# A two-layer decoder step in fp32: how the convolution's taps are spread over the stages, which units stand beside a layer's first blocks, and narrower attention operands

## The chip, the core and the metric

The kernel runs on one core of one Trainium2 chip. The metric is the device time of one execution in microseconds (us), as the median of several runs. The engines are named as in the profile: PE (TensorE matmul) and PEld (its weight loads), DVE (VectorE), ACT (ScalarE), POOL (GpSimd) and SP (SyncE, which issues DMAs).

## What is computed

One inference step of a decoder with two layers, for a prompt of 1024 tokens and 8 sampled sequences of 4 tokens: 1056 token columns in all, model width 1024, everything in float32. Cut to what matters here:

```
h = rms(x)*(1+scale) + shift                       # scale, shift from an adaLN product
u_a, bch, glu, q, k, v, mgate, mrg = split(h @ w_in)
y_a = pooled means over windows 2/4/8/16, minus self, times w_pool          # A
y_b = B * dwconv3(C * h_b)                                                   # B
y_c = silu(layernorm(dwconv31(val*sigmoid(gl)) + b))                         # C
w   = softmax(q1 k1) - lam * softmax(q2 k2);  y_d = rms(w @ v)               # D, causal, 4 heads
merged = sum_n sigmoid(mrg_n) * ((y_n * silu(mgate_n)) @ w_branch_n)
x = x + gate * rms(merged @ w_o)
```

`lam` is exp(lq0.lq1) - exp(lq2.lq3) + a constant, from a small input. The samples attend to 1024 cached tokens each, and the convolutions and the pooling take their past rows from small state inputs.

## The kernel before

**Products.** Channels lie on the 128 partitions and tokens along the free axis, in three blocks of 352 columns (the last holds 320 prompt columns and the 32 sample columns). Each fp32 operand is split into a high part (copied to the fp32r format, L208 for weights on ACT) and a remainder (L209 on DVE); a product is three matmul series, high*high, high*low and low*high (`three`), so an item of eight 128-row slices is 24 matmuls of 352 columns (`gemm`, L236). A *unit* is one 128-channel slice of the input projection for all three blocks, so three items. `Ring` loads a unit's weights two ahead and splits them into three pairs of buffers (whi, wlo); `rmain.dest` can name other tiles for a unit.

**Order.** `drive` runs a list of units: for each item the matmuls, then the evaluation of its PSUM block, one `step_side` (two more inside the item) and `fills[n % len(fills)]` calls of `step_fill`. `side` holds generators whose work is laid between the items: one attention head (`attn`), the decoding of two heads (`decode`), `pool`, `layernorm`. `fill` holds the taps of branch C. Each engine runs its instructions in one fixed order, so an instruction that waits holds up all behind it.

**A layer.** `layer` first runs the first head's K, V and Q units for blocks 0 and 1, then starts `attn(0)`, runs block 2 of the three units, and goes on with the gate of branch D (`mgd(0)`) and branch B. The previous layer's output projection makes the third block's input last: its sum of squares (`sumsq`, L366 to L373: ACT squares, DVE `tensor_reduce`), the reciprocal root (`rstd_of`, whose matmul is L354), and `norm_apply` (L388 DVE, L389 ACT, L390 DVE). In layer 0 `rstd_x` does the sum of squares by eight fp32 matmuls with ones (L1260). `setup_lambda` loads the input of `lam` into the tile `od` (L417), and its exponential is L420 on ACT. The heads 1 to 3 follow in turn with the rest of branch B beside them; the last is attention 3.

**Attention.** For a query block of 128 rows `a_part` makes scores S for two maps (q, k: matmul, mask matmul, remainder matmul with `kl`), the row maximum (L582), the exponential (L585) and the difference of the two maps. The columns of a chunk are at least 256 (`chunks`). `t_part` transposes the weights, and `pv` (L614) multiplies pairs of query blocks by V; where the first block of a pair can see nothing of a key block, a memset puts zeros there. At the end L351 to L362 normalise the head.

**Branches A and C.** `ev_val` makes the convolution's input, and `conv` appends 32 entries per channel slice c to `fill`: `samples`, then 31 taps, each one DVE instruction over 128x1024 (L947). The units gl(0) to gl(2) come first, then four pairs `ua(c)`, `mga(c)` (the pooling units, each with `pool(c)`: window sums on POOL L1006, DVE L1013, ACT L1014, DVE L1015, three small products, L1023 to L1025), then gl(3). `FR = (2,)`: two fills per item in all of them and in the merges. After gl(3) the loop runs fills until no `samples` stands in front and not all 32 entries of slice 3 are left. The four merges follow in the order A, B, D, C; what is left in `fill` runs in the first one and at its end (`drain_fill`). The layer norm of branch C (L1081, L1084, L1088) runs beside the third merge.

```
            if sides:
                step_side()
            step_fill(fills[n % len(fills)])
...
        drive(first, order=[(u, b) for b in range(2) for u in range(3)], begun=begun)
        side.append(attn(0))
        drive(first, order=[(u, 2) for u in range(3)])
        drive([mgd(0), uc_(0), uh(0), ub(0)])
```

## Time and profile before

| | |
|---|---|
| median of 3 runs | 2972.73 us (2972.08 to 2975.25) |
| the profiled execution | 2971.34 us, span of its work 2969.6 us |
| PE busy | 2882.3 us, 97% |
| DVE, ACT, POOL busy | 1618.5, 1060.0, 483.1 us (55%, 36%, 16%) |
| mean granted TensorE clock | 0.989 of full speed |

An engine's busy time is the time in which one of its instructions ran. Times in rows count from the start of the span. A matmul's own duration in a row holds a latency that overlaps with its neighbours; what it takes of PE is the distance from its start to the next start. The granted clock of a stretch is the mean over it, 1.00 being the upper of the two levels and 0.5 the lower.

### The profile page before, as it was taken

The page shows a single profiled execution, that of the slowest core. Times are in us where ns is not written, and L with a number is a line of the kernel's source. Part 1 is how long each engine was busy: PE and PEld are TensorE (multiplying, and loading weights), DVE is VectorE, ACT ScalarE, POOL GpSimd, SP SyncE. Part 2 cuts the span into 40 slices and gives each one's busy share as a digit, 9 for nine tenths or more (in the row PEclk, how much of TensorE's full clock was granted, in tenths as well). Part 3 has the DMA queues.
Part 4 walks back from the last instruction along what each step waited for, and adds up shares of the span by engine and source line. Part 5 has one row for each costly group of instructions (what it writes and reads, how often), then busy time and mean ns, then how long its engine had stood idle before and what let it go on. Part 6 is the DMA issues. An engine that isn't in the chain of part 4 may idle for free.

```text
span 2969.6 us, 45889 instructions
## 1 busy us (share of the span) xinstructions
PE 2882.3 (97%) x18198; PEld 2774.0 (93%) x18198; DVE 1618.5 (55%) x2488; ACT 1060.0 (36%) x2086; POOL 483.1 (16%) x632
## 2 busy tenths in 40 slices
PE   7999999999999999999979999999999999999997
PEld 5999898999899999999979988988999999999997
DVE  5766366489952145323487653675799422543233
ACT  5565256322112133213455652653221121322132
POOL 1121010113100111011230110201140001220123
PEclk9999999999999999999999999999999999999999
DMA  6114621551232233222321245116411221221122
GB/s 237 51 58 134 186 64 39 177 158 45 81 110 101 72 104 102 79 72 72 111 97 48 73 148 174 57 36 198 141 41 60 81 72 50 77 87 58 50 70 98
DMA packets 135960, 280.06 MB, mean 94 GB/s; under 512 B 18338, under 2 KB 88994, under 8 KB 134210
## 3 DMA queue, kind: packets, MB, share of 16 engines
q10 hardware_dynamic: 45072, 145.74, 15.7%
q1 hardware_dynamic: 79778, 90.73, 9.6%
q0 software_dynamic: 10896, 40.67, 3.7%
q8 instruction: 143, 2.34, 0.3%
q14 instruction: 71, 0.58, 0.1%
HBM read 240.73 MB, written 36.34 MB: 93 GB/s over the span
## 4 chain that ended last, share of the span: by engine, by line
PE 80%; DVE 7%; ACT 5%; DMA 3%; SPq 3%; issue 2%; POOL 0%; ACTq 0%; DVEq 0%; POOLq 0%
PE mm_t L236 42%; PE m_t L236 28%; PE s_t L236 3%; DVE acc_t L947 2%; SPq L664 2%; PE ms_t L236 2%; PE ms_t L603 1%; DMA e_t<-in_kc_dram 1%; ACT rop_t L489 1%; SPq L401 1%; DVE wlo_t L209 1%; PE s_t L769 1%; PE s_t L695 1%; PE ada_t L298 1%; PE ms_t L1260 1%
## 5 line engine op out<-in xcount | busy, mean ns | idle before, releaser
L236 PE MATMUL mm_t<-hh_t,whi_t 128*128 128x352 f32 x2792 | 528.9, 327 | 10.8 <-ACT hh_t L383 4.8
L236 PE MATMUL mm_t<-hh_t,wlo_t 128*128 128x352 f32 x2792 | 528.6, 326 | 0.0
L209 DVE TENSOR_TENSOR wlo_t<-wst_t,whi_t 128x1024 fp32r<-128x1024 f32 x203 | 269.2, 1330 | 475.9 <-ACT whi_t L208 475.3
L236 PE MATMUL mm_t<-hl_t,whi_t 128*128 128x352 f32 x2792 | 525.3, 325 | 0.0
L236 PEld LDWEIGHTS mm_t<-hh_t,whi_t 128*128 128x128 f32 x2792 | 460.2, 190 | 22.9 <-issue 7.5
L236 PEld LDWEIGHTS mm_t<-hl_t,whi_t 128*128 128x128 f32 x2792 | 462.0, 189 | 11.2 <-issue 10.0
L236 PEld LDWEIGHTS mm_t<-hh_t,wlo_t 128*128 128x128 f32 x2792 | 463.0, 190 | 4.1 <-issue 3.3
L947 DVE SCALAR_TENSOR_TENSOR acc_t<-uc_t,vec_t,acc_t 128x1024 f32<-128x1024 f32 x240 | 319.2, 1346 | 2.0
L208 ACT ACTIVATE whi_t<-wst_t 128x1024 fp32r<-128x1024 f32 x203 | 213.4, 1056 | 275.6 <-PE mm_t L236 194.1
L1158 POOL TENSOR_TENSOR mg_t<-mg_t,th_t 128x352 f32<-128x352 f32 x144 | 145.3, 1011 | 932.9 <-DVE th_t L1157 932.7
L236 PE MATMUL m_t<-hh_t,wlo_t 128*128 128x352 f32 x1352 | 248.5, 325 | 0.0
L236 PE MATMUL m_t<-hl_t,whi_t 128*128 128x352 f32 x1352 | 248.2, 325 | 0.0
L236 PE MATMUL m_t<-hh_t,whi_t 128*128 128x352 f32 x1352 | 246.1, 324 | 0.7 <-DVE ga_t L979 0.7
L236 PEld LDWEIGHTS m_t<-hh_t,wlo_t 128*128 128x128 f32 x1352 | 224.3, 190 | 0.6
L236 PEld LDWEIGHTS m_t<-hl_t,whi_t 128*128 128x128 f32 x1352 | 224.2, 190 | 0.2
L236 PEld LDWEIGHTS m_t<-hh_t,whi_t 128*128 128x128 f32 x1352 | 222.9, 189 | 1.0 <-DVE ga_t L979 1.0
L1065 ACT ACTIVATE th_t<-m_t 128x352 f32<-128x352 f32 x114 | 52.7, 463 | 376.3 <-PE m_t L236 372.4
L1065 ACT ACTIVATE th_t<-mm_t 128x352 f32<-128x352 f32 x78 | 36.0, 463 | 262.3 <-PE mm_t L236 254.4
L585 ACT ACTIVATE e_t<-s_t,sml_t 128x256 f32<-128x256 f32 (+7 forms) x128 | 94.2, 739 | 51.7 <-DVE sml_t L583 50.7
L582 DVE TENSOR_REDUCE sml_t<-s_t 128x1 f32<-128x256 f32 (+7 forms) x128 | 94.0, 751 | 12.4 <-PE s_t L236 11.6
L236 PE MATMUL m_t<-yh_t,whi_t 128*128 128x352 f32 x460 | 94.6, 326 | 0.0
L236 PE MATMUL m_t<-yl_t,whi_t 128*128 128x352 f32 x460 | 93.2, 324 | 0.0
(361 smaller groups left out, 3928.0 us busy)
## 6 DMA issues: line engine op xcount, KB each, us to landing
wst_t<-in_wst_dram ACTq DMA_DIRECT2D x209, 512.0 KB, 3.7
e_t<-in_kc_dram SPq DMA_DIRECT2D x224, 128.0 KB, 2.9
e_t<-in_vc_dram SPq DMA_DIRECT2D x216, 128.0 KB, 2.8
rld_t<-ysp_t ACTq DMA_DIRECT2D x16, 528.0 KB, 4.1
wa_t<-in_wada_dram SPq DMA_DIRECT2D x16, 512.0 KB, 9.2
wlo_t<-in_wada_dram ACTq DMA_DIRECT2D x16, 512.0 KB, 3.7
whi_t<-in_wada_dram ACTq DMA_DIRECT2D x16, 512.0 KB, 4.3
x_t<-in_xT_dram SPq DMA_DIRECT2D x3, 1408.0 KB, 12.9
```

The source lines that it names most:

```text
L208: sc.activation(out=R(hi), in_=st, func=AF.Copy)
L209: (eng or ve).tensor_tensor(out=R(lo), in0=st, in1=hi, op=ALU.subtract)
L236: last_mm[0] = m = te.matmul(out=out, lhsT=R(lh), rhs=R(rh), start=first and i == 0, stop=last and i == n - 1)
L298: te.matmul(out=acc[c:c + 32], lhsT=scs[:, k], rhs=w, start=k < 4, stop=k >= 4)
L401: r = sp.value_load(pt[0:1, i:i + 1], min_val=0, max_val=NPOOL - 1)
L489: sc.activation(out=sw[32 * (g ^ 1):32 * (g ^ 1) + 32], in_=pb[32 * g:32 * g + 32], func=AF.Copy)
L582: ve.tensor_reduce(out=s[:, j:j + 1], in_=S[j][:, :n], axis=AX.X, op=ALU.max)
L585: sc.activation(out=E[qb % 2][j][:, :n], in_=S[j][:, :n], func=AF.Exp, bias=s[:, 2 + j:3 + j], scale=0.125, accum_out=s[:, 4 + j:5 + j])
L664: sp.dma_start(out=buf[:, j * 256:(j + 1) * 256], in_=cache[l][bass.ds(r, 1), p].rearrange("a p n -> p (a n)"))
L947: pace(ve.scalar_tensor_tensor(out=a, in0=v, scalar=w(k), in1=a, op0=ALU.mult, op1=ALU.add))
L1065: sc.activation(out=th[:, b * TB:(b + 1) * TB], in_=pb, func=AF.Tanh, scale=0.5)
L1158: gp.tensor_tensor(out=mg[:, d, cl], in0=mg[:, d, cl], in1=th, op=ALU.add)
```

## The change

Seven edits, in one diff:

- `fold` replaces every `tensor_reduce` over the middle axis by two `tensor_tensor` additions (704 and 352 columns), in `sumsq` and twice in `layernorm`; `rstd_x` does blocks 1 and 2 so, with one fp32 matmul in place of eight.
- `mgd(0)` becomes the fourth unit of the first group: after blocks 0 and 1 of K, V and Q come the three items of `mgd(0)`, then block 2 of K, V and Q. The weights of `mgd(0)` go to the tiles `od` and `e7`. While it runs, `attn(0)` stops before its third query block.
- A chunk of S takes only the columns it has; `pv` multiplies only the 128 live columns for the last key block of a pair, and its memsets go.
- `od` and `ms` change places in `decode`, and `od` is allocated in `pv(0)`, the tiles e4 to e7 in the first `t_part`.
- Sample columns of branch C have their own tile and DMA.
- Two fills per item stay in the gl units; one in the pooling units; 3, 2, 3 for the items of a unit in the merges.
- The loop after gl(3) runs only while a `samples` entry stands in front, which `appendleft` now puts there as soon as it exists.

```diff
@@ -362,13 +362,17 @@
-    def sumsq(x, t, acc):
+    def fold(t, out, first=None):
+        h = t[:, 0:2] if first is None else first
+        ve.tensor_tensor(out=h, in0=t[:, 0:2], in1=t[:, 2:4], op=ALU.add)
+        ve.tensor_tensor(out=out, in0=h[:, 0], in1=h[:, 1], op=ALU.add)
+    def sumsq(x, ts, acc):
...
-            k = slice(4 * i, 4 * i + 4)
-            o = t[:, k] if t.shape[1] == KC else t
-            sc.activation(out=o, in_=x[:, k], func=AF.Square)
-            ve.tensor_reduce(out=acc[:, i], in_=o.rearrange("p k n -> p n k"), axis=AX.X, op=ALU.add)
+            sc.activation(out=ts[i], in_=x[:, 4 * i:4 * i + 4], func=AF.Square)
+            fold(ts[i], acc[:, i])
@@ -551,10 +555,9 @@
-            wt = [ep(f"e{4 + i}", 4, 256) for i in range(4)]
-            od = ep("od", 1056)
-            qz = ep("ms", 1024)[:, 0:512].rearrange("p (i j q) -> p i j q", i=2, j=2)
+            wt, od = [], []
+            qz = ep("ms", 1056)[:, 0:512].rearrange("p (i j q) -> p i j q", i=2, j=2)
@@ -566,7 +569,7 @@
-                chunks = [slice(c0, c0 + min(512, max(n - c0, 256))) for c0 in range(0, n, 512)]
+                chunks = [slice(c0, min(c0 + 512, n)) for c0 in range(0, n, 512)]
@@ -591,10 +594,9 @@
             def t_part(qb):
+                if qb == 0:
+                    wt.extend(ep(f"e{4 + i}", 4, 256) for i in range(4))
...
-                if qb % 2 == 0:
-                    for lo in range(2):
-                        gp.memset(wtp(lo, qb + 1)[:, 0:P], 0.0)
@@ -607,17 +609,23 @@
-                pr = []
-                for k in range(2 * s + 2):
-                    pr += [(vh[:, k], wtp(0, k)), (vh[:, k], wtp(1, k)), (vl[:, k], wtp(0, k))]
-                gemm(pb, pr)
-                sc.activation(out=od[:, s * 256:s * 256 + 256], in_=pb, func=AF.Copy)
+                pr = [(v, lo, k) for k in range(2 * s + 2) for v, lo in ((vh, 0), (vh, 1), (vl, 0))]
+                pr = pr[:-4] + pr[-3:] + pr[-4:-3]
+                for i, (v, lo, k) in enumerate(pr):
+                    c = slice(P if k == 2 * s + 1 else 0, 256)
+                    gemm(pb[:, c], [(v[:, k], wtp(lo, k)[:, c])], first=i == 0, last=i == len(pr) - 1)
+                if s == 0:
+                    od.append(ep("od", 1056)[:, :SEQ])
+                sc.activation(out=od[0][:, s * 256:s * 256 + 256], in_=pb, func=AF.Copy)
...
                 while qb >= 5 and kqdone[h] < 2 or qb >= 7 and not vdone[h]:
+                    yield
+                while qb == 2 and held:
                     yield
@@ -856,18 +864,23 @@
-        first = kvq(0)
+        gq = Pool(f"gq{l}", LEFT, reuse_waits="tile")
+        first = kvq(0) + [mgd(0)]
+        rmain.dest[pos[first[3][0]]] = [ep(t, n)[:, 0:1024] for t, n in (("od", 1056), ("e7", 1024))]
+        held.append(True)
...
+        drive(first, order=[(3, 0), (3, 1), (3, 2)])
+        held.clear()
...
-        gq = Pool(f"gq{l}", LEFT, reuse_waits="tile")
-        drive([mgd(0), uc_(0), uh(0), ub(0)])
+        drive([uc_(0), uh(0), ub(0)])
@@ -928,34 +941,38 @@
             def samples():
-                a = st["a"] = cpool("acc", T)
+                a = cpool("smp", NS)
...
-                    ve.tensor_reduce(out=a[:, SEQ + i:SEQ + i + 16], in_=prd, axis=AX.X, op=ALU.add)
-                ve.tensor_scalar(out=a[:, SEQ:], in0=a[:, SEQ:], scalar1=cv("b_cconv", l, c), scalar2=None, op0=ALU.add)
+                    ve.tensor_reduce(out=a[:, i:i + 16], in_=prd, axis=AX.X, op=ALU.add)
+                ve.tensor_scalar(out=a, in0=a, scalar1=cv("b_cconv", l, c), scalar2=None, op0=ALU.add)
+                gp.dma_start(out=csp[l, c, :, SEQ:], in_=a)
...
                 def f():
-                    a, v = st["a"][:, 0:SEQ], u[:, k:k + SEQ]
+                    if k == 0:
+                        st["a"] = cpool("acc", SEQ)
+                    a, v = st["a"], u[:, k:k + SEQ]
...
-                        gp.dma_start(out=csp[l, c], in_=st["a"])
+                        gp.dma_start(out=csp[l, c, :, 0:SEQ], in_=a)
...
-            fill.append((c, samples))
+            fill.appendleft((c, samples))
...
-        FR = (2,)
+        FC, FA, FM = (2,), (1,), (3, 2)
...
-        drive(gl(0) + gl(1) + gl(2), 1, FR)
+        drive(gl(0) + gl(1) + gl(2), 1, FC)
@@ -1028,16 +1045,16 @@
-        drive([ua(0), mga(0)], 1, FR)
+        drive([ua(0), mga(0)], 1, FA)
...
-            drive([ua(c), mga(c)], 1, FR)
-        drive(gl(3)[:1], 1, FR)
+            drive([ua(c), mga(c)], 1, FA)
+        drive(gl(3)[:1], 1, FC)
...
-        drive(gl(3)[1:], 1, FR)
+        drive(gl(3)[1:], 1, FC)
...
-        while fill and fill[0][1].__name__ == "samples" or sum(t == 3 for t, _ in fill) == 32:
+        while fill and fill[0][1].__name__ == "samples":
@@ -1078,14 +1095,14 @@
-                ve.tensor_reduce(out=s1, in_=x.rearrange("p k n -> p n k"), axis=AX.X, op=ALU.add)
+                fold(x, s1, t[:, 0:2])
...
-                ve.tensor_reduce(out=s2, in_=t.rearrange("p k n -> p n k"), axis=AX.X, op=ALU.add)
+                fold(t, s2)
@@ -1137,7 +1154,7 @@
-                    drive([win(O_MRG + n * D, 2 * dp + x, ev_mrg(ths[x]))], 1, FR)
+                    drive([win(O_MRG + n * D, 2 * dp + x, ev_mrg(ths[x]))], 1, FM)
@@ -1253,15 +1270,20 @@
-            for i in range(2):
-                tx = su("tx", 4, TB, bufs=2)
-                sc.activation(out=tx, in_=xb0[b][:, 4 * i:4 * i + 4], func=AF.Square)
-                for k in range(4):
-                    te.matmul(out=pb, lhsT=ones, rhs=tx[:, k], start=i + k == 0, stop=i + k == 4)
+            ts = [su("tx", 4, TB, bufs=2) for _ in range(2)]
+            if b == 0:
+                for i in range(2):
+                    sc.activation(out=ts[i], in_=xb0[b][:, 4 * i:4 * i + 4], func=AF.Square)
+                    for k in range(4):
+                        te.matmul(out=pb, lhsT=ones, rhs=ts[i][:, k], start=i + k == 0, stop=i + k == 4)
+            else:
+                te.matmul(out=pb, lhsT=ones, rhs=sumsq(xb0[b], ts, accs[b]), start=True, stop=True)
...
-            ve.scalar_tensor_tensor(out=t, in0=pb, scalar=-3.0, in1=y, op0=ALU.add, op1=ALU.mult)
+            rs = t if b < 2 else pb
+            ve.scalar_tensor_tensor(out=rs, in0=pb, scalar=-3.0, in1=y, op0=ALU.add, op1=ALU.mult)
+            return rs
```

**PE at the start of layer 0**, from the transposes of V's block 1 (L518, now L522) on; `s_t` are scores, `maskr_t` is the mask, `od_t` the tile for the weights of `mgd(0)`. Before:

```order
L518 MATMUL ms_t<-cs_t,vcm_t 128x128 x3
L236 MATMUL mm_t<-hh_t,whi_t 128x352 x8
L236 MATMUL mm_t<-hh_t,wlo_t 128x352 x8
L236 MATMUL mm_t<-hl_t,whi_t 128x352 x8
L236 MATMUL s_t<-k_t,q_t 128x256
L236 MATMUL s_t<-maskr_t,identr_t 128x128
```

With the change:

```order
L522 MATMUL ms_t<-cs_t,vcm_t 128x128 x5
L236 MATMUL s_t<-k_t,q_t 128x128
L236 MATMUL s_t<-maskr_t,identr_t 128x128
L236 MATMUL s_t<-k_t,q_t 128x128
L236 MATMUL s_t<-maskr_t,identr_t 128x128
L236 MATMUL s_t<-kl_t,ms_t 128x128 x2
L236 MATMUL mm_t<-hh_t,od_t 128x352 x16
```

Block 2 of K followed the transposes; now the first scores and 16 matmuls with the weights in `od` do.

**ACT at the start of layer 1**, from the last block's `norm_apply` (`hh_t`) on; `lamt_t` is the exponential for `lam`. Before:

```order
L389 ACTIVATE hh_t<-ob_t,modT_t 128x320 x5
L572 ACTIVATE ms_t<-q_t 64x128 x4
L420 ACT_TABLE_LOAD
L420 ACTIVATE lamt_t<-lamt_t 128x2
L489 ACTIVATE rop_t<-mm_t 32x352 x4
L208 ACTIVATE whi_t<-wst_t 128x1024
```

With the change:

```order
L393 ACTIVATE hh_t<-ob_t,modT_t 128x320 x5
L575 ACTIVATE ms_t<-q_t 64x128 x6
L588 ACT_TABLE_LOAD
L588 ACTIVATE e_t,sml_t<-s_t,sml_t 128x128
L424 ACTIVATE lamt_t<-lamt_t 128x2
L208 ACTIVATE od_t<-wst_t 128x1024
```

The copy that makes the weights of `mgd(0)` stands behind the last block's `hh`, a table load, the first exponential of the scores and that of `lam`.

**ACT where attention 3 of layer 0 begins and attention 2 is normalised** (`od_t`, L351 to L360); L585, now L588, is the exponential of the scores. Before:

```order
L351 ACTIVATE e_t<-e_t 128x512
L489 ACTIVATE rop_t<-mm_t 32x352 x4
L208 ACTIVATE whi_t<-wst_t 128x1024
L359 ACT_TABLE_LOAD
L359 ACTIVATE e_t<-ms_t,epsc_t 128x512
L572 ACTIVATE ms_t<-q_t 64x128
L585 ACT_TABLE_LOAD
L585 ACTIVATE e_t,sml_t<-s_t,sml_t 128x128
L360 ACTIVATE e_t<-e_t 128x512
L572 ACTIVATE ms_t<-q_t 64x128
L183 DMA wst_t<-in_wst_dram 128x1024
L359 ACT_TABLE_LOAD
```

With the change:

```order
L351 ACTIVATE e_t<-e_t 128x512
L359 ACT_TABLE_LOAD
L359 ACTIVATE e_t<-ms_t,epsc_t 128x512
L360 ACTIVATE e_t<-e_t 128x512
L502 ACTIVATE q_t<-rop_t 64x352 x2
L493 ACTIVATE rop_t<-mm_t 32x352 x4
L208 ACTIVATE whi_t<-wst_t 128x1024
L575 ACTIVATE ms_t<-q_t 64x128 x2
L359 ACTIVATE e_t<-ms_t,epsc_t 128x512
L588 ACT_TABLE_LOAD
L588 ACTIVATE e_t,sml_t<-s_t,sml_t 128x128 x2
L360 ACTIVATE e_t<-e_t 128x512
```

Both roots (L359) now stand ahead of both exponentials, with one table load for each kind.

## Rows read from the trace of the kernel before

**Rows 1.** The page: the span, PE's busy time and share, and the chain that ended last.

```profile
span 2969.6 us, 45889 instructions
PE 2882.3 (97%) x18198; PEld 2774.0 (93%) x18198; DVE 1618.5 (55%) x2488; ACT 1060.0 (36%) x2086; POOL 483.1 (16%) x632
...
PE 80%; DVE 7%; ACT 5%; DMA 3%; SPq 3%; issue 2%; POOL 0%; ACTq 0%; DVEq 0%; POOLq 0%
```

**Rows 2.** PE's waits: what it wanted to run, who released it, us in total, how often, the longest.

```profile
PE s_t L236 <- ACT e_t L585: 11.3, 8, 3.2
PE ms_t L236 <- ACT dh_t L1014: 9.4, 2, 5.3
...
PE ms_t L1084 <- DVE ls_t L1081: 2.0, 3, 1.1
```

**Rows 3.** Stretches of the span: their length, then the busy time of PE, PEld, DVE, ACT and POOL (with instructions), the granted clock, the DMA share and GB/s.

```profile
470.00:482.00 12.00, 7.30 (x34) 6.04 (x33) 10.30 (x30) 8.71 (x25) 0.68 (x2) 0.72 0.13 47
700.00:770.00 70.00, 62.93 (x372) 61.75 (x371) 69.17 (x61) 16.55 (x32) 29.74 (x25) 0.95 0.16 49
770.00:919.00 149.00, 149.00 (x927) 144.79 (x926) 95.04 (x102) 23.89 (x39) 2.21 (x4) 1.00 0.27 92
1940.00:1956.00 16.00, 10.26 (x50) 8.65 (x49) 11.55 (x32) 12.70 (x31) 0.68 (x2) 0.79 0.19 67
2195.00:2245.00 50.00, 43.56 (x249) 42.44 (x248) 49.86 (x47) 11.31 (x22) 17.61 (x15) 0.93 0.16 55
```

**Rows 4.** PE's timeline in attention 2 of layer 0, at full clock: start, duration, line, operation. 24 products of `pv` (256 columns) run from the first row to the one at 456.86; behind them come the first scores of attention 3.

```profile
454.02 0.40 PE L236 MATMUL ms_t<-e_t,vh_t 128*128 128x256 f32 x2
...
456.86 1.46 PE L236 MATMUL mm_t<-hh_t,wlo_t 128*128 128x352 f32 x8
...
461.31 0.22 PE L236 MATMUL s_t<-maskr_t,identr_t 128*128 128x128 f32 x1
461.37 0.34 PE L236 MATMUL s_t<-kl_t,ms_t 128*128 128x256 f32 x1
```

**Rows 5.** PE's timeline at the start of layer 0. In brackets: the idle time ahead and who ended it.

```profile
33.60 4.89 PE L1260 MATMUL ms_t<-tx_t,ones_t 128*128 128x352 f32 x16
...
70.99 0.90 PE L518 MATMUL ms_t<-cs_t,vcm_t 128*128 128x128 f32 x3 [4.44 <-ACT vcm_t L533]
71.55 2.69 PE L236 MATMUL mm_t<-hh_t,whi_t 128*128 128x352 f32 x8
```

**Rows 6.** DVE's timeline where layer 1 begins.

```profile
1528.98 0.88 DVE L1215 TENSOR_TENSOR xb_t<-xb_t,ob_t 128x704 f32<-128x704 f32 x1
...
1530.21 5.05 DVE L371 TENSOR_REDUCE acc_t<-ob_t 128x352 f32<-128x1408 f32 x2
...
1536.27 0.53 DVE L372 TENSOR_TENSOR acc_t<-acc_t 128x352 f32<-128x352 f32 x1
...
1546.39 3.78 DVE L390 SCALAR_TENSOR_TENSOR hl_t<-ob_t,modT_t,hh_t 128x320 fp32r<-128x320 f32 x8
1553.38 0.29 DVE L418 TENSOR_TENSOR od_t<-od_t 128x128 f32<-128x128 f32 x1 [3.21 <-DMA od_t<-in_lamqk_dram]
```

**Rows 7.** ACT's timeline at the start of layer 0.

```profile
76.51 1.02 ACT L498 ACTIVATE k_t<-rop_t 64x352 fp32r<-64x352 f32 x2
78.20 1.85 ACT L489 ACTIVATE rop_t<-mm_t 32x352 f32<-32x352 f32 x4 [0.68 <-PE mm_t L236]
80.08 1.06 ACT L208 ACTIVATE whi_t<-wst_t 128x1024 fp32r<-128x1024 f32 x1
```

**Rows 8.** PE's timeline where layer 1 begins, beside rows 6.

```profile
1537.37 0.66 PE L354 MATMUL ms_t<-parts_t,ones_t 128*128 128x352 f32 x1 [7.70 <-ACT parts_t L351]
...
1545.13 4.08 PE L236 MATMUL mm_t<-hh_t,whi_t 128*128 128x352 f32 x15 [4.84 <-ACT hh_t L383]
1549.05 1.43 PE L236 MATMUL mm_t<-hh_t,wlo_t 128*128 128x352 f32 x8
...
1556.72 1.56 PE L236 MATMUL mm_t<-hh_t,whi_t 128*128 128x352 f32 x8 [2.02 <-DVE rop_t L490]
```

**Rows 9.** ACT's timeline where attention 3 of layer 0 begins: its table loads.

```profile
463.39 1.28 ACT L359 ACT_TABLE_LOAD   x1
...
465.59 1.28 ACT L585 ACT_TABLE_LOAD   x1
...
468.21 1.28 ACT L359 ACT_TABLE_LOAD   x1
...
471.83 1.28 ACT L585 ACT_TABLE_LOAD   x1
```

**Rows 10.** PE's timeline there.

```profile
473.63 0.58 PE L236 MATMUL s_t<-k_t,q_t 128*128 128x256 f32 x1 [3.20 <-ACT e_t L585]
```

**Rows 11.** POOL's timeline at the last pooling unit of layer 0: the end of its window sums.

```profile
746.87 0.48 POOL L1010 TENSOR_TENSOR sa_t<-sa_t,cs_t 128x15 f32<-128x15 f32 x1
```

**Rows 12.** DVE's timeline behind it.

```profile
757.75 0.18 DVE L1013 SCALAR_TENSOR_TENSOR sa_t<-sa_t,ua_t 128x32 f32<-128x32 f32 x1
```

**Rows 13.** The taps (L947) alone: length of the stretch, DVE's busy time with their count, clock, DMA share, GB/s.

```profile
700.00:770.00 70.00, 41.51 (x28) 0.95 0.16 49
770.00:919.00 149.00, 61.87 (x50) 1.00 0.27 92
```

More of the change, by code (lines that the diff above doesn't have):

```diff
@@ L431, in layer @@
     def layer(l, pos, hh, hl, begun, psB):
-        vdone, gdone, kqdone = [False] * NH, [False] * NH, [0] * NH
+        vdone, gdone, kqdone, held = [False] * NH, [False] * NH, [0] * NH, []
         def weights(i, n=P):
@@ L632, in attn @@
                 yield
-            o = od[:, :SEQ]
+            o = od[0]
             for i in range(2):
@@ L701, in decode @@
                 yield
-            pt_ = ep("od", 1056)
-            dsm = ep("ms", 1024)
+            pt_ = ep("ms", 1056)
+            dsm = ep("od", 1056)
             wd = dsm[:, 0:512].rearrange("p (g n) -> p g n", g=8)
@@ L755, in pads @@
                 return w
-            load(ep("od", 1056)[:, 0:1024])
+            load(ep("ms", 1056)[:, 0:1024])
             nw = [pads(pg) for pg in range(3)]
@@ L1217, in layer @@
                 gp.dma_start(out=xmid[b], in_=xb)
-                rs = rstd_of(sumsq(xb, ob, op("acc", 2, TB)), 1.0 / D, two(op("parts", 2, TB)), two(op("yt", 2, TB)))
+                rs = rstd_of(sumsq(xb, [ob[:, 0:4], ob[:, 4:8]], op("acc", 2, TB)), 1.0 / D, two(op("parts", 2, TB)), two(op("yt", 2, TB)))
                 for t, x in zip(nh, "hl"):
@@ L1283, in step_kernel @@
             pos.append(po)
-        rstd_x(0)
+        rss = [rstd_x(0)]
         ada_first(0, psA("mm", 512))
@@ L1298, in first_half @@
         def first_half(b):
-            norm_apply(0, b, xb0[b], xb0[b], accs[b][:, 0], h[0][b], h[1][b], HALVES[0])
+            norm_apply(0, b, xb0[b], xb0[b], rss[b], h[0][b], h[1][b], HALVES[0])
             for u in range(3):
@@ L1305, in step_kernel @@
         first_half(0)
-        rstd_x(1)
+        rss.append(rstd_x(1))
         first_half(1)
@@ L1310, in step_kernel @@
         make_A(0, 4, 4)
-        rstd_x(2)
+        rss.append(rstd_x(2))
         su.close()
         for b in range(3):
-            norm_apply(0, b, xb0[b], xb0[b], accs[b][:, 0], h[0][b], h[1][b], HALVES[1] if b < 2 else range(KC))
+            norm_apply(0, b, xb0[b], xb0[b], rss[b], h[0][b], h[1][b], HALVES[1] if b < 2 else range(KC))
         sx.close()
```

## The prediction

> **What bounds the kernel now.** I read the page first: PE is busy for 2882.3 of 2969.6 us, and the chain that ended last runs through PE for 80% [rows 1]. So only three things can change the time: fewer columns through PE, fewer PE waits, and less time at the lower clock. Then PE's waits: the reader is to see that the largest entries are few in number and sit in a few places, the scores behind the exponential (11.3 us in 8 waits) and the pooling products behind `dh` (9.4 us in 2) [rows 2]. Then the stretches around them: each such wait also brings the granted clock down, to a mean of 0.72 over 12 us, 0.95 over 70, 0.79 over 16 and 0.93 over 50, that is 3.4, 3.5, 3.4 and 3.5 us lost besides the wait [rows 3]. Last the timelines of PE and of the engine it waits for, at each place. The profiled execution took 2971.34 us; I sum against that, and the median of the runs, 2972.73, lies 1.4 us above it.
>
> **Narrower operands.** Per head, `pv` has 4 pairs with 3 products on the last key block: 12 in each of 8 head passes, 96, go from 256 to 128 columns. The chunks of query blocks 0 and 4 end in 128 columns: 2 blocks, 2 maps, 2 products, 8 passes make 64 more. 24 products of 256 columns took 2.84 us, 118 ns each, and a 128-column mask product 60 ns to the next start [rows 4]. 160 x 58 ns is **-9.3 us**, all on PE's path. The bounds are -9.3 and 0, the latter if a product this narrow waits for its own weight load when several follow each other; the row shows one among wider ones, and I take the row.
> The Trainium skill (TensorE: Matmul & The Clock Gate, Back-to-back issue gap) says against this that a stream of weight load and 128-column matmul sustains about 81 ns each; the row's single mask product, at 60 ns, does not show that. By the page's figure the saving would be an estimated 5.9 us and the sum below -24.9.
>
> **Start of layer 0.** `rstd_x` for blocks 1 and 2 drops 14 of 16 fp32 matmul instructions; 16 take 4.89 us [rows 5], so 8.6 us leave PE. They buy little, because PE then waits for something later. The two folds and a sum on DVE (2 x (0.88 + 0.53) + 0.53 = 3.35 us by the same shapes [rows 6]) stand in for 4.89 us, so block 2 is ready about 1.5 us sooner. Before, PE ran block 2 of K from 71.55, at the lower clock (8 matmuls in 2.69 us against 1.46) [rows 4, 5], which is worth a full-speed start at 73.4. Now 16 products with weights in `od` stand there, and everything on PE queues behind them. Their ACT copy follows the K copies that end at 77.53, then four small copies, a table load and the exponential for `lam`: about as long as what lay between there and the copy at 80.08 before [rows 7]. So `od` is ready near 80.08 + 1.06 - 1.5 = 79.6. PE idles from about 70 to then, starts at the lower clock (1.7 us lost, half of what such a stretch costs [rows 3]) and has 0.4 us of scores done: worth 80.9. That is 7.5 us later than 73.4; I take **+7**. Ends: +11 without the 1.5 and with twice the clock loss, -3 if the copy keeps up with the transposes.
>
> **Start of layer 1.** Two reductions (5.05 us) become two folds (2.82), and the second matmul of the preceding root stands 12 rather than 29 matmuls behind its first (17 x 0.16 = 2.7 us): the last block comes 4.9 us sooner [rows 4, 6]. PE's wait of 7.70 shrinks by that [rows 8]. But the DMA for `lam` into `od` waits for the last read of the tile whose memory `od` takes, the end of L390 at 1550.17, and DVE gets it 3.21 us later at 1553.38 [rows 6]. Less 4.9 that is 1548.5; two DVE instructions, the exponential and the copy (1.06 [rows 7]) put the weights at 1550.4. With 1.7 us of lower clock and less the 0.4 of scores: worth 1551.7. Before, block 2 started at 1545.13, its first 15 matmuls took 4.08 us instead of 2.4, and a wait of 2.02 followed [rows 8]: worth 1548.8. **+3**; ends -2 (the DMA lands while PE is still at the scores) and +8 (the 4.9 do not arrive).
>
> **Attention 3, both layers.** ACT loads four tables in 9 us, alternating between the root and the exponential, and the exponentials stand behind them; PE waits 3.20 us at 473.63 alone [rows 9, 10]. In the new order both roots precede both exponentials, two loads (2.6 us) go, and PE has 40 matmuls (6.4 us) between the first scores and the next that need their PSUM. ACT still has some 9 us of work between them, so I leave about 1.5 us of wait per layer: 11.3 falls to 3, and the clock loss from 6.8 to 2. **-13**; ends -18 (all goes) and -4 (only the loads).
>
> **Pooling units, both layers.** POOL has the last window sums ready at 747.35, and DVE takes them up only at 757.75 [rows 11, 12]. DVE is busy for 69.17 of 70 us there, 41.51 of it on 28 taps of 1.48 us [rows 3, 13]: a queue that is 10 us late. One fill instead of two in 24 items takes 24 taps, 35 us, out of the stage, and the burst after gl(3) goes too. The waits for `dh` (9.4) should go and with them 7.0 us of clock [rows 2, 3]; I keep 1.4 as a remainder, since in the new order two taps and a weight split still stand between the last gate and `dh`. **-15**; ends -19 (smaller waits for PSUM go too) and -5.
>
> **First merge.** 66 taps remain for it instead of 42, and 72 fills are there for them. 24 x 1.24 us [rows 13] raise DVE from 95.04 to 125 of 149 us [rows 3]: 84%. PE runs without a gap there now; an item there is 12 matmuls, 1.94 us, and with five PSUM buffers an eviction may be four items, 7.7 us, late, more than three taps take (3.7 us). **0**, at most +6. The reloads behind the merge need the memory of the last taps, and the next merge gives them two units of 11.6 us.
>
> **The rest.** In the layer norm the folds end PE's wait for `ls` (2.0 [rows 2]): **-1**, ends -2 and +1. The 64 memsets on an engine that is busy 16% [rows 1], the samples' own tile and DMA, and the exchange of `od` and `ms` lie beside other work: 0; with that cover gone they would show as POOL releasing PE, which no large wait does now [rows 2].
>
> Sum: -9.3 + 7 + 3 - 13 - 15 + 0 - 1 = -28.3, so 2943.0 against the profiled execution and **2944 us** against the median. About 0.2%, 6 us, is what a measurement here can tell from no change.
>
> **Rivals.**
> - *The weights in `od` come in time* and `mgd(0)` covers both starts, as a gate that needs no attention could. Then PE runs on from 72 and from 1541: -7 and -8 instead of +7 and +3, in all -53.3, **2919**. The orders of ACT and SP speak against it: the copy stands behind table, exponential and DMA. Chance 0.10.
> - *Narrow products do not pay*: the first term is 0 and the time **2954**. For it: the weights of each product stay 128x128. Against: the 60 ns [rows 4]. The Trainium skill's figure, named above, would give 2948. Chance 0.15.
> - *The waits change their releaser only*: ACT remains late at attention 3 and the pooling keeps its stalls since POOL's sums, `dh` and the weight split still follow each other. The gains there fall to their ends, -4 and -5 instead of -13 and -15, in all -9.3, **2963**. Against it: the 10.4 us for which the sums lie ready [rows 11, 12]. Chance 0.15.
> - *DVE becomes the bound in the first merge*, and the kernel is slower. Without taps DVE has 33.2 us of work there (95.04 - 61.87); 66 taps fit into 149 us up to 1.755 us each, and beyond that PE's evictions wait for DVE. At 2.2 us a tap, 178 us, it is 29.6 us over in each layer: 2971.3 - 28.3 + 59 + 1.4, about **3003**. For it: a tap takes 1.48 us where POOL is at work [rows 13]. Against: POOL is busy for 2.21 of 149 us there [rows 3]. Chance 0.10.
>
> **How the numbers follow.** The forecast has 0.50, with its own range 2932 to 2958. The range for 8 in 10 leaves out the first and the last rival, 0.2 together, and reaches over the third: 2926 to 2968. Faster by over 0.2% (below 2966.8): the forecast, the first two rivals and about a third of the third rival, 0.80. Within 0.2%: the rest of the third, 0.09. Slower: the last rival and a little for both starts at their upper ends with the gains at their lower ones, 0.11.
>
> **What would show it.** Columns: PE's `pv` products in two shapes, with 60 ns between starts for the narrow ones. Starts: a wait of `mm_t` for `od_t` (ACT L208) of 6 to 10 us in layer 0 and 4 to 8 in layer 1, with a lowered clock; if it is missing, the first rival holds. Attention 3: the exponential's entry at 3 us or less, clock near 1.00 there. Pooling: DVE near 60% busy, no `dh` entry above 1.5 us, clock 1.00. First merge: DVE near 84%, PE without a gap. The prediction is wrong if PE waits for DVE inside that merge, if the waits of the pooling return under another releaser, or if the starts lose more than 20 us together.

## The result: 2957.9 us, 0.9946 of the time before

| | before | after |
|---|---|---|
| median | 2973.99 us (2972.08 to 2977.68) | 2957.89 us (2955.13 to 2961.46) |
| ratio, 95% interval | | 0.9946 [0.9934, 0.9958] |
| profiled execution, its span | 2971.34, 2969.6 us | 2961.46, 2959.7 us |
| mean granted clock | 0.989 | 0.988 |

The change saves 16 us; 28 were forecast. The profiled execution of after is the slowest of its four, so its span differs from before's by only 10 us. In experiments 2 and 11 one execution each, of some 7300 us, is left out. The page of after, against [rows 1]:

```profile
span 2959.7 us, 45764 instructions
PE 2873.8 (97%) x18170; PEld 2768.7 (94%) x18170; DVE 1606.5 (54%) x2516; ACT 1055.7 (36%) x2078; POOL 476.9 (16%) x576
```

PE's waits of after, against [rows 2]: what it wanted to run, who released it, us in total, how often, the longest.

```profile
PE s_t L236 <- ACT ms_t L575: 9.1, 3, 7.3
PE s_t L236 <- ACT e_t L588: 6.1, 2, 5.9
PE ms_t L522 <- DVE vl_t L526: 5.2, 3, 2.3
...
PE s_t L236 <- DVE q_t L505: 3.0, 1, 3.0
PE mm_t L236 <- ACT od_t L208: 2.6, 1, 2.6
...
PE ms_t L354 <- ACT parts_t L351: 2.3, 1, 2.3
```

The entry for `dh` (9.4 us) is gone, and of the exponential's 6.1 us the one wait of 5.9 lies elsewhere than before, at the start of layer 1. Of the entries shown, the first, the fourth and the fifth are new, all at the two starts; the third, for V, was 0.6 us before. Stretches of after, against [rows 3] (columns as there; the first is the start of layer 0, the second and last are attention 3):

```profile
60.00:100.00 40.00, 27.84 (x148) 26.59 (x147) 25.99 (x63) 26.25 (x64) 11.80 (x18) 0.79 0.16 55
470.00:490.00 20.00, 16.53 (x93) 15.05 (x92) 16.42 (x44) 15.11 (x40) 1.62 (x3) 0.91 0.16 54
700.00:770.00 70.00, 70.00 (x437) 70.00 (x436) 61.72 (x62) 20.02 (x38) 30.06 (x24) 1.00 0.15 49
766.00:915.00 149.00, 149.00 (x927) 144.79 (x926) 118.94 (x120) 24.44 (x40) 3.28 (x6) 1.00 0.29 96
1525.00:1555.00 30.00, 13.85 (x60) 12.28 (x59) 21.07 (x53) 15.92 (x41) 5.99 (x11) 0.60 0.11 40
1940.00:1960.00 20.00, 16.76 (x97) 15.27 (x96) 16.87 (x45) 15.33 (x40) 1.61 (x3) 0.91 0.16 54
2195.00:2245.00 50.00, 50.00 (x312) 50.00 (x311) 45.46 (x47) 12.21 (x22) 19.34 (x16) 1.00 0.15 45
```

The pooling stretches (700:770, 2195:2245) and the first merge (766:915) show a PE without a gap at full clock. The two starts show a PE that is idle for 12 and 16 us. Before, it was idle for under 5 us in the first of these stretches:

```profile
60.00:100.00 40.00, 35.37 (x207) 34.75 (x206) 35.29 (x76) 33.66 (x78) 18.40 (x33) 0.91 0.28 91
```

PE at the start of layer 0, after (start, duration; in brackets the idle time and who ended it), against [rows 5]:

```profile
71.15 0.90 PE L522 MATMUL ms_t<-cs_t,vcm_t 128*128 128x128 f32 x3 [4.68 <-ACT vcm_t L537]
75.06 0.44 PE L236 MATMUL s_t<-k_t,q_t 128*128 128x128 f32 x1 [3.01 <-DVE q_t L505]
...
81.69 5.06 PE L236 MATMUL mm_t<-hh_t,od_t 128*128 128x352 f32 x16 [2.64 <-ACT od_t L208]
```

ACT's timeline ahead of that product:

```profile
78.23 0.94 ACT L575 ACTIVATE ms_t<-q_t 64x128 fp32r<-64x128 f32 x3
79.19 1.28 ACT L424 ACT_TABLE_LOAD   x1
80.48 0.20 ACT L424 ACTIVATE lamt_t<-lamt_t 128x2 f32<-128x2 f32 x1
80.59 1.04 ACT L208 ACTIVATE od_t<-wst_t 128x1024 fp32r<-128x1024 f32 x1
```

PE at the start of layer 1, after, against [rows 8]:

```profile
1538.95 0.81 PE L236 MATMUL s_t<-kl_t,ms_t 128*128 128x128 f32 x2 [7.29 <-ACT ms_t L575]
1545.66 0.58 PE L236 MATMUL s_t<-k_t,q_t 128*128 128x256 f32 x1 [5.90 <-ACT e_t L588]
...
1546.70 5.06 PE L236 MATMUL mm_t<-hh_t,od_t 128*128 128x352 f32 x16
```

DVE and ACT ahead of that product:

```profile
1544.56 0.29 DVE L422 TENSOR_TENSOR od_t<-od_t 128x128 f32<-128x128 f32 x1 [2.83 <-DMA od_t<-in_lamqk_dram]
```

```profile
1545.15 0.37 ACT L588 ACTIVATE e_t<-s_t,sml_t 128x128 f32<-128x128 f32 x1 [3.28 <-DVE sml_t L586]
...
1545.60 1.04 ACT L208 ACTIVATE od_t<-wst_t 128x1024 fp32r<-128x1024 f32 x1
```

In layer 0 the first product of `mgd(0)` waits for its weights, which ACT copies last. In layer 1 the same lateness stands under other names: PE waits for two small results of ACT, and the weights arrive while it does. DVE waits for the DMA of `lam`, ACT's exponential for DVE, and the copy stands behind the exponential. Both times 16 products then take 5.06 us, twice what they take at the upper clock (16 x 161 ns = 2.6).

### The profile page after: what moved, and what is told of

The parts are those of the page before. It is cut to its first block, busy times and chain, and to the rows that moved or that the text cites. A ratio compares the mean times of both kernels' runs of the same rounds, so it can differ in the third digit from the quotient of the medians.

```text
span 2959.7 us, 45764 instructions
## 1 busy us (share of the span) xinstructions
PE 2873.8 (97%) x18170; PEld 2768.7 (94%) x18170; DVE 1606.5 (54%) x2516; ACT 1055.7 (36%) x2078; POOL 476.9 (16%) x576
## 5 line engine op out<-in xcount | busy, mean ns | idle before, releaser
L236 PE MATMUL mm_t<-hh_t,whi_t 128*128 128x352 f32 x2744 | 520.5, 327 | 7.2 <-DVE rop_t L494 3.4
L236 PE MATMUL mm_t<-hh_t,wlo_t 128*128 128x352 f32 x2744 | 516.5, 325 | 0.0
L236 PE MATMUL mm_t<-hl_t,whi_t 128*128 128x352 f32 x2744 | 515.2, 325 | 0.0
L236 PEld LDWEIGHTS mm_t<-hh_t,whi_t 128*128 128x128 f32 x2744 | 451.0, 189 | 21.0 <-issue 8.3
L236 PEld LDWEIGHTS mm_t<-hh_t,wlo_t 128*128 128x128 f32 x2744 | 453.9, 189 | 6.1 <-issue 5.0
L236 PEld LDWEIGHTS mm_t<-hl_t,whi_t 128*128 128x128 f32 x2744 | 453.2, 189 | 6.2 <-issue 5.0
L585 DVE TENSOR_REDUCE sml_t<-s_t 128x1 f32<-128x256 f32 (+7 forms) x128 | 95.1, 752 | 41.6 <-PE s_t L236 40.6
L588 ACT ACTIVATE e_t<-s_t,sml_t 128x256 f32<-128x256 f32 (+7 forms) x128 | 94.4, 740 | 59.9 <-DVE sml_t L586 55.0
```

The lines of the kernel that those rows point to most:

```text
L236: last_mm[0] = m = te.matmul(out=out, lhsT=R(lh), rhs=R(rh), start=first and i == 0, stop=last and i == n - 1)
L585: ve.tensor_reduce(out=s[:, j:j + 1], in_=S[j][:, :n], axis=AX.X, op=ALU.max)
L588: sc.activation(out=E[qb % 2][j][:, :n], in_=S[j][:, :n], func=AF.Exp, bias=s[:, 2 + j:3 + j], scale=0.125, accum_out=s[:, 4 + j:5 + j])
```

## Experiments

All ratios are to the kernel before, run beside each kernel (its medians lay at 2973.8 to 2974.3 us).

**1. `mgd(0)` back behind block 2** (on the changed kernel).

```diff
-        first = kvq(0) + [mgd(0)]
-        rmain.dest[pos[first[3][0]]] = [ep(t, n)[:, 0:1024] for t, n in (("od", 1056), ("e7", 1024))]
-        held.append(True)
+        first = kvq(0)
...
-        drive(first, order=[(3, 0), (3, 1), (3, 2)])
-        held.clear()
...
-        drive([uc_(0), uh(0), ub(0)])
+        drive([mgd(0), uc_(0), uh(0), ub(0)])
```

> The changed kernel with the first gate unit back at its old place, behind block 2 of K, V and Q, with weights in the ring's own buffers; all else as changed. My theory: the two layer starts cost 13.6 us in the changed kernel (9.4 in layer 0, 4.2 in layer 1, by the distance of the same decode products in the two traces), so this takes that back: about 13 us below the changed kernel, 29 below the kernel before, ratio 0.990. The terms of the prediction (+7, +3) would make it 10 below the changed kernel. Rival, the gate unit covers the starts and the loss is elsewhere: no faster than the changed kernel, ratio 0.9946 or above.

Measured: 2941.12 us (2939.49 to 2943.35), 0.9891 [0.9876, 0.9906]. The move costs 16.8 us. PE at the start of layer 0 in this kernel:

```profile
70.82 0.90 PE L522 MATMUL ms_t<-cs_t,vcm_t 128*128 128x128 f32 x3 [4.68 <-ACT vcm_t L537]
71.37 2.69 PE L236 MATMUL mm_t<-hh_t,whi_t 128*128 128x352 f32 x8
73.86 2.46 PE L236 MATMUL mm_t<-hh_t,wlo_t 128*128 128x352 f32 x8
```

Its stretches at the two starts, for the rows 60:100 and 1525:1555 above:

```profile
60.00:100.00 40.00, 33.95 (x197) 32.51 (x196) 33.24 (x78) 34.12 (x81) 16.43 (x25) 0.91 0.29 94
1517.00:1547.00 30.00, 21.43 (x113) 20.08 (x112) 23.56 (x55) 21.29 (x49) 10.19 (x16) 0.77 0.19 53
```

Block 2 of K follows the transposes at once, since its weights have long been there: PE is busy for 33.95 instead of 27.84 us at a mean clock of 0.91 instead of 0.79. Its first 16 products are no faster than those with the weights in `od` (2.69 and 2.46 us against 5.06); they begin at 71.37 and not at 81.69. Between the same products the move costs 8.5 us in layer 0 and 8.0 in layer 1 (from 1508.31 to 1640.80 with the change, from 1499.72 to 1624.22 here).

**2. The move by itself**: experiment 8's kernel, which has the new tiles and nothing else of the change, with `mgd(0)` in the first group (the lines of experiment 1 the other way round).

> The kernel of e6 (tiles only) with the first gate unit moved ahead of block 2 of K, V and Q and its weights in od and e7, as in the change; no folds, taps or narrower products. My theory: the move costs by itself what taking it back gave, 16.8 us, from e6's 2966 to about 2983, ratio 1.003, slower than the kernel before. Rival, it costs only together with the earlier sums: 2966 to 2970, ratio 0.997 to 0.999.

Measured: 2983.02 us, 1.0029 [1.0019, 1.0039], 17.0 us above experiment 8. One sign, one size, on two very different kernels. Its PE waits:

```profile
PE mm_t L236 <- ACT od_t L208: 9.6, 2, 6.8
```

**3. The input of `lam` in another tile than the weights** (on the changed kernel), so that no DMA into `od` stands ahead of the copy.

```diff
-        setup_lambda(l, ep("od", 1056)[:, 0:4 * HD]...)
+        setup_lambda(l, qp_("tbb", T)[:, 0:4 * HD]...)
```

> The changed kernel with the small input for lam loaded into the head of the tile tbb, not into od, so that the weights of the first gate unit need not wait for it; ACT's copy into od then stands right behind block 1's V in layer 0 and right behind the last block's hh in layer 1. My theory (the wait for od is what the starts cost): the copy ends 3.5 us earlier in layer 0 and 4 in layer 1, about 7 us below the changed kernel, ratio 0.992. If the lam input is not what holds the copy: no change, ratio 0.9946. If the gate unit then covers the whole start: 20 us below the changed kernel, ratio 0.988.

Measured: 2954.31 us, 0.9934 [0.9921, 0.9948]: 3.6 us gained where 7 were expected. ACT's copy in layer 1:

```profile
1542.98 1.06 ACT L208 ACTIVATE od_t<-wst_t 128x1024 fp32r<-128x1024 f32 x1 [2.91 <-issue]
```

It moved up from 1545.60 by 2.6 us only, 1.0 of them gained ahead of the start (the product at 1508.31 with the change stands at 1507.31), and then waits for nothing that is named. `od` lies over the memory of the last block's `ob`, which DVE reads until 1542.89; experiment 4 tests that. In layer 0 next to nothing is gained: the copy comes at 78.99 instead of 80.59, but the table load and the exponential for `lam` now stand ahead of V's copy, so the transposes wait longer (4.68 us with the change):

```profile
73.02 0.90 PE L522 MATMUL ms_t<-cs_t,vcm_t 128*128 128x128 f32 x3 [6.19 <-ACT vcm_t L537]
```

**4. `od` over another piece of memory** (on experiment 3): two tiles allocated ahead move `od` off that buffer.

```diff
+        ep("e0", 1024), ep("e1", 1024)
         setup_lambda(l, qp_("tbb", T)[:, 0:4 * HD]...)
```

> The fourth kernel (lam's input in tbb) with two tiles named ahead of od, so that od and e7 lie over memory of the previous layer that block 1 read last, not block 2. In the fourth kernel the copy into od waited 2.9 us in layer 1 for that memory. My theory (each thing that holds the copy costs PE directly): the copy ends near 1540 instead of 1544.0 in layer 1, layer 0 stays, so about 4 us below the fourth kernel, 2950, ratio 0.992. Rival, the first rival of the prediction: with the weights early the gate unit covers the starts and the time falls to 2935 or below, ratio 0.987. Rival, memory is not what holds it: 2954, ratio 0.9934.

Measured: 2952.69 us, 0.9924 [0.9911, 0.9938]. ACT and PE in layer 1:

```profile
1538.34 2.35 ACT L393 ACTIVATE hh_t<-ob_t,modT_t 128x320 fp32r<-128x320 f32 x5
1540.60 1.04 ACT L208 ACTIVATE od_t<-wst_t 128x1024 fp32r<-128x1024 f32 x1
```

```profile
1541.69 4.66 PE L236 MATMUL mm_t<-hh_t,od_t 128*128 128x352 f32 x16 [9.51 <-ACT od_t L208]
```

The copy now runs the moment ACT is through with the last block's `hh`, and PE has idled 9.5 us by then. The two memory waits together are worth 5.2 us; how this divides (3.6 and 1.6 by the medians) is not told from noise. Between the same products of layer 1 experiments 3 and 4 give back 1.2 and 3.3 of the 8.0 us that the move costs there (1507.31 to 1638.59, 1507.93 to 1635.94), and in layer 0 none of the 8.5. That the rest is ACT's order, in which the copy stands behind `hh` and behind the copies of V and K, is argued and not shown: a version with the copy ahead of them was not tried.

**5. The taps alone** (on the kernel before): the numbers of fills, samples in front, their own tile, no burst.

```diff
-        FR = (2,)
+        FC, FA, FM = (2,), (1,), (3, 2)
...
-            fill.append((c, samples))
+            fill.appendleft((c, samples))
...
-        while fill and ... == "samples" or sum(t == 3 for t, _ in fill) == 32:
+        while fill and fill[0][1].__name__ == "samples":
```

> The kernel before with only the taps redistributed (2 fills in the gl units, 1 in the pooling units, 3-2-3 in the merges, no burst, sample columns in their own tile). My theory: this is the whole of the pooling gain, 15 us (7.5 per layer), ratio 0.995, the wait for dh gone, clock 1.00 from 700 to 770, DVE near 80% in the first merge with PE without a gap. Rival, the gain in the pooling stage came with the other edits: under 5 us, ratio above 0.998. Rival, DVE is the bound in the first merge: slower.

Measured: 2952.63 us, 0.9932 [0.9918, 0.9945]: -21.2 us, against 15 forecast. Its stretches have PE busy for 70.00 of 70 us and 149.00 of 149, DVE for 64.46 and 116.66, all at a clock of 1.00, and the wait for `dh` is not in its list.

**6. Still more taps in the merge** (on experiment 1): every second item of the pooling units none, seven per two items in the merges.

```diff
-        FC, FA, FM = (2,), (1,), (3, 2)
+        FC, FA, FM = (2,), (1, 0), (4, 3)
```

> The kernel of e1 with 12 more taps moved out of the pooling units into the first merge (fills 1 and 0 by turns there, 4 and 3 in the merges): 78 taps in the merge. My theory: DVE has 33 us of other work and 78 x 1.28 us of taps there, 133 of 149 us (89%), still below the bound; the pooling stage has no wait left to win, so within 2 us of e1, ratio 0.989. Rival, the last rival of the prediction, DVE bounds the merge and PE's evictions wait: slower than e1 by 5 us or more, with PE waits on DVE between 766 and 915 us.

Measured: 2941.24 us (2937.83 to 2943.93), 0.9890 [0.9874, 0.9905], the same as experiment 1. Its first merge, columns as above:

```profile
758.00:907.00 149.00, 149.00 (x927) 144.79 (x926) 129.85 (x130) 24.12 (x39) 3.27 (x6) 1.00 0.28 95
```

With 78 taps, DVE at 87%, PE still has no gap. The rival in which DVE becomes the bound there is rejected at the change's 66 to 68 taps and ten beyond.

**7. Narrower operands alone** (on the kernel before): the `chunks` and `pv` hunks of the diff, without the memsets.

> The kernel before with only the narrower attention operands (chunks of S, 128 live columns in pv, no memsets). From the changed kernel's trace: a narrow product behind another takes 111 ns to the next start, only the first of a group 60, so the 160 cost as much as their weight loads; my theory now is 2.5 us, ratio 0.999. The prediction's term says 9.3 us, ratio 0.997; 81 ns each would give 5.9 us, ratio 0.998.

Measured: 2972.06 us, 0.9997 [0.9988, 1.0006]: -1.8 us; neither 9.3 nor 5.9 lies in the interval. The end of a `pv` series in this kernel:

```profile
456.06 0.57 PE L236 MATMUL ms_t<-e_t,vh_t 128*128 128x256 f32 x4
456.47 0.45 PE L236 MATMUL ms_t<-e_t,vl_t 128*128 128x128 f32 x2
456.75 1.46 PE L236 MATMUL mm_t<-hh_t,wlo_t 128*128 128x352 f32 x8
```

From the first `pv` product at 453.93 to the last row's start, 24 products take 2.82 us, against 2.84 with 256 columns throughout [rows 4].

**7b. A quarter of those columns** (on experiment 7, one run; the kernel leaves out 96 of the 128 live queries of those products).

```diff
-                    c = slice(P if k == 2 * s + 1 else 0, 256)
+                    c = slice(224 if k == 2 * s + 1 else 0, 256)
```

> The kernel of e3 with pv's products on the last key block of a pair cut from 128 to 32 columns, which leaves out 96 of the 128 live queries there. My theory: a product this narrow behind another waits for its own weights, so the starts of a group of three stay 60, 111 and 111 ns apart as with 128 columns, and the time stays that of e3, 2972. Rival, the columns set the pace: the later starts come closer by up to 40 ns (96 columns at 2.4 per ns), 96 x 40 ns = 3.8 us less.

Measured: 2971.34 us, one run. The same place:

```profile
457.87 0.53 PE L236 MATMUL ms_t<-e_t,vh_t 128*128 128x256 f32 x4
458.24 0.47 PE L236 MATMUL ms_t<-e_t,vl_t 128*128 128x32 f32 x2
458.55 1.46 PE L236 MATMUL mm_t<-hh_t,wlo_t 128*128 128x352 f32 x8
```

Medians from start to next start, for the three narrow products and the wide one behind them: 61, 110, 112, 173 ns with 128 columns; 28, 111, 112, 205 with 32. Both add up to some 456 ns, against 3 x 117 + 120 = 471 with 256. Fewer columns shorten only the first of a series, and the wide product behind gives that back: what passes at a steady 111 ns whatever the columns is the weight load, one per product. PEld's rows at this place, two loads in 0.23 us; with 128 columns two take 0.22 (456.41 to 456.63):

```profile
458.21 0.30 PEld L236 LDWEIGHTS ms_t<-e_t,vl_t 128*128 128x128 f32 x2
458.44 0.31 PEld L236 LDWEIGHTS mm_t<-hh_t,wlo_t 128*128 128x128 f32 x2
```

**8. The tiles alone** (on the kernel before): `od` in the first `pv`, e4 to e7 in the first `t_part`, `od` and `ms` exchanged in `decode`.

> The kernel before with only the tiles changed: od allocated in the first pv, e4 to e7 in the first transposing step, od and ms exchanged in decode. ACT's order then has 42 table loads instead of 50, as in the changed kernel. My theory: this edit alone, which the prediction put at 0, is what reorders ACT at attention 3; by the distances in the traces it gives 4.4 us in layer 0 and 1.7 in layer 1 and costs about 2 in new DMA waits of decode, in all 4 us, ratio 0.9986. The prediction's term for attention 3 would make it 13, ratio 0.9956. Rival, the reordering needs the narrower products as well: no change.

Measured: 2966.02 us, 0.9971 [0.996, 0.9981]: -8.3 us, where I expected 4 and the prediction had 13 (its line on the exchange said 0). ACT's order has 42 table loads instead of 50; experiments 5 and 7 keep 50. So the tiles make the new order at attention 3; the later allocation and the exchange in `decode` were not tried apart. Its two stretches there, columns as above:

```profile
470.00:490.00 20.00, 17.05 (x94) 16.15 (x93) 14.63 (x42) 10.86 (x33) 0.68 (x2) 0.83 0.22 73
1940.00:1960.00 20.00, 17.01 (x91) 16.15 (x91) 14.33 (x39) 11.44 (x34) 0.68 (x2) 0.83 0.22 77
```

PE is still idle for 3 us in each, and the clock falls. By the same products in the traces, attention 3 with the decoding around it gives 2.6 us in layer 0 (from 361 to 691 us of before) and 1.3 in layer 1 (1761 to 2178), near the 4 that I had expected; the span is 5.5 us shorter.

**9. The folds alone** (on the kernel before): the `fold` hunks in `sumsq` and `layernorm`.

> The kernel before with only the folds in the output projection's sum of squares and in the layer norm (not in layer 0's first sums). My theory: what the other parts leave of the gate-back kernel's gain: 32.7 - 21 - 8.3 - 1 = 2.4 us, about 1 in the layer norm's waits and the rest at the start of layer 1, ratio 0.999. The prediction's working would give 2.2 us at the start of layer 1 from the folds and 1 in the layer norm, 3.2. Rival, no place of it is on the path: 1.000.

Measured: 2966.58 us, 0.9976 [0.9967, 0.9985]: -7.6 us, where I expected 2.4. The root behind them in layer 1, against the wait of 7.70 in [rows 8]:

```profile
1533.88 0.43 PE L354 MATMUL ms_t<-parts_t,ones_t 128*128 128x352 f32 x1 [2.34 <-ACT parts_t L351]
```

In the trace 4.8 us of it lie at the start of layer 1 and 2.5 us in the two layer norms; elsewhere it loses 2.6 against the trace of before, so the span is 4.7 us shorter. The folds alone also bring the second matmul of the preceding root from 29 to 12 matmuls behind its first, so the prediction's figure for them is 4.9 + 1 and not the 3.2 above.

**10. Eight matmuls again in `rstd_x`** (on experiment 1).

```diff
-            if b == 0:
+            if b < 3:
```

> The kernel of e1 with the sums of squares of blocks 1 and 2 in layer 0 made by eight fp32 matmuls each again, the folds kept elsewhere. My theory: PE then has 8.6 us more matmuls there, but waits for the last block's normalisation anyway; block 2 comes at most 1.5 us later, so 0 to +1.5 us against e1, 2941 to 2943, ratio 0.9891 to 0.9896. Rival, the matmuls lie on the path: +8, ratio 0.992.

Measured: 2940.18 us, 0.9881 [0.9866, 0.9896], against 2941.12. The folds in layer 0 buy nothing. In experiment 1 PE waits for their sum instead, and then for V (4.68 us, as shown there):

```profile
PE ms_t L1276 <- DVE acc_t L376: 2.9, 1, 2.9
```

**11. The best of these** (experiments 1, 6 and 10 together).

> The kernel of e8 (gate unit back, 12 more taps in the first merge) with the eight matmuls of e7 in layer 0. Both were the same as e1 within their intervals, so about 2940, ratio 0.989; below 2937 would mean that both help a little.

Measured: 2939.29 us, 0.9881 [0.9865, 0.9896]. It beats both kernels, by 35 and 19 us, but not experiment 1 by more than the measurement tells.

## Why the prediction was right in sign and promised 12 us too much

| term | forecast | by the medians | by the profiled spans | from |
|---|---|---|---|---|
| narrower operands | -9.3 | -1.8 | +0.5 | 7 |
| `mgd(0)` first, gross | +16.4 | +16.8, +17.0 | +19.3, +16.2 | 1, 2 |
| folds, start of layer 0 | -1.5 | +0.9 | -0.2 | 10 |
| folds, start of layer 1 and layer norm | -5.9 | -7.6 | -4.7 | 9 |
| attention 3 | -13 | -8.3 | -5.5 | 8 |
| taps: pooling and first merge | -15 | -21.2 | -19.4 | 5 |

The forecasts add up to the prediction's -28.3. The measured 2957.9 us lies at the very end of its own range (2932 to 2958), and only since misses of both signs partly cancel: without what the taps gave beyond their forecast it would lie outside. The gross +16.4 is what the prediction's two starts hold for the move once its own savings there are taken out again: 7 + 1.5 for layer 0, 3 + 4.9 for layer 1.

- **Narrower operands failed as a step.** "I take the row" chose a single mask product with wider ones around it, 60 ns, for products that follow each other. Those start 110 ns apart (experiments 7, 7b), so the lower bound that the prediction named, a wait for the weight load, was the value; the second rival holds, and at least 7.5 us of the forecast were not there. The Trainium skill (TensorE: Matmul & The Clock Gate, Back-to-back issue gap) has about 81 ns for each product of a sustained stream of weight load and 128-column matmul. This kernel measures 111 ns, and the 5.9 us estimated from the page's figure lie outside the interval. The direction of the page's figures, that a narrow product does not get cheaper in proportion, was right.
- **The starts were right in mechanism**, and by the same products in both traces layer 0 loses 8.8 us (forecast 7) and layer 1 4.0 (forecast 3; 1512.65 to 1641.12 before, 1508.31 to 1640.80 after). In layer 0 the copy came at 80.59 (forecast 78.5, behind the very instructions named). The 1.5 us by which the folds were to bring block 2 sooner did not come: the transposes start at 71.15, before at 70.99 [rows 5]. (The 16 of 4.89 us [rows 5] are one block's eight fp32 matmuls, two instructions each; the 8.6 us count both blocks.) The loss at the lower clock was put too low on both sides: 1.9 us before and 1.7 after, where the first 16 products lose some 2.2 in experiment 1 and 2.5 in after.
- **The sign of the starts was badly chosen.** The wait of `mm_t` for `od` is 2.6 us in layer 0, where I looked for 6 to 10, and in layer 1, where I looked for 4 to 8, there is none. The idle time stands under ACT L575 and L588, which ACT does right ahead of the copy, and under DVE L505. The rival that `mgd(0)` covers both starts is rejected for this change: even without the two memory waits (experiments 3, 4) PE still idles 9.5 us in layer 1.
- **The folds** were right at the start of layer 1 (4.8 of 4.9 us) and small by 1.5 in the layer norm, and in layer 0 they give nothing (experiment 10). My own 2.4 for experiment 9 was worse than the prediction's figure.
- **Attention 3 failed in part as a mechanism**, by 5 us or more. The exponential's waits went, as forecast (0.2 us of the 11.3 remain outside the start of layer 1), but not the idleness: PE's next wait there is for V, in layer 0 of after as follows, and the clock is still 0.91 over 20 us, 1.8 us per layer, where I had written 2 in all.

```profile
482.06 0.55 PE L522 MATMUL ms_t<-cs_t,vcm_t 128*128 128x128 f32 x3 [2.28 <-DVE vl_t L526]
483.32 0.61 PE L522 MATMUL ms_t<-cs_t,vcm_t 128*128 128x128 f32 x3 [0.71 <-DVE sml_t L586]
```

  The wait for V was small before:

```profile
PE ms_t L518 <- DVE vl_t L522: 0.6, 1, 0.6
```

  PE's waits where attention 3 of layer 0 begins add up to 5.4 us before (0.9, 3.2 and 1.3) and to 3.3 after (0.3, 2.3 and 0.7), with a new one of 1.1 for `sml` ahead of them, at 445.2. So the third rival, that the waits change their releaser only, holds here in substance, with DVE as the releaser. The cause was placed wrongly too: the working treats the new order as given and the tiles as worth 0; experiment 8 shows that the tiles make the order.
- **Pooling was under-sized by 4 to 6 us.** The queue of DVE was the cause: the sums that lay ready for 10.4 us [rows 11, 12] are now taken up after 2.4.

```profile
750.52 0.21 POOL L1027 TENSOR_TENSOR sa_t<-sa_t,cs_t 128x15 f32<-128x15 f32 x1
```

```profile
753.13 0.18 DVE L1030 SCALAR_TENSOR_TENSOR sa_t<-sa_t,ua_t 128x32 f32<-128x32 f32 x1
```

  The remainder of 1.4 us that I kept was not there, and the smaller waits went as well. But DVE is at 88% of the stretch (61.72 of 70), not near 60%: 21 taps remain of 28, and each takes 1.59 us (33.29 / 21) instead of 1.48. A queue does not have to be short to be in time, only not to grow.
- **First merge: right.** 68 taps take 86.98 us, 1.28 each (forecast 1.24); DVE is busy for 80% (forecast 84%), and PE has no gap.

**What stays open.** By the medians the four parts without the move add up to 1.8 + 7.6 + 8.3 + 21.2 = 38.9 us, and together (experiment 1) they give 32.7. By the spans of the profiled executions they add up to -0.5 + 4.7 + 5.5 + 19.4 = 29.1 us, against 29.2 for experiment 1 (2969.6 to 2940.4). So the traces show no overlap between the parts. The profiled execution of before, at 2971.34 us, lies 2.5 to 3.0 us under its medians beside the experiments, so the sum of the four medians counts that four times and experiment 1 once; the profiled executions of the four parts lie within 0.7 us of their medians. A single part is therefore known to some 3 us only, and which of the two columns is nearer stays open. Executions of one kernel also spread by some us: the four of after lie at 2955.1, 2955.4, 2960.4 and 2961.5 us. In the profiled one, the slowest, PE waits 11.2 us for the decoding's DMAs (`in_kc`, `in_vc`), in experiment 1's 7.9; that this makes the spread is not shown.

## What to carry to other kernels

Work that is laid into a gap needs everything of its own early, weights and the memory they go to included: look up where the copy that makes them stands in the order of its engine, and not only whether the arithmetic needs the late result. A price read off one instruction among wider ones does not hold for a series of them; look for a row with two in succession, or take the bound. And the tiles that a step names, and when it allocates them, can decide the order of another engine's work: judge such an edit by the order it gives, not by its lines. Last, a wait that goes can leave its time to the next one in line: look up what PE would wait for then.

## What the chip showed that I had not expected

- A fp32 matmul of 128 or 32 columns behind another takes 110 to 112 ns to the next start; 256 columns take 117, 352 take 161. With a new 128x128 weight for each, narrowing below 256 is worth about 5% of a product.
- A reduction over the middle axis (128x352 from 128x1408) takes DVE 2.5 us, 5.05 for two [rows 6]; two additions over the same data (L368 and L369 of after, 0.88 + 0.52) take 1.40.
- The same tap takes DVE 1.59 us in the pooling units, where POOL is busy for 30.06 of 70 us, and 1.28 us in the merge, where POOL is busy for 3.28 of 149. That POOL is the reason was not tested.
